# Four gate tiles of a delta-net mixer moved behind the scan, the scan's output kept in SBUF

## The chip, the cores and the metric

One core of one Trainium2 chip runs the whole program. The metric is the device time of one execution in microseconds (us); three runs of the kernel before gave 3149.6 us as median (3138.0 to 3154.76). TensorE (PE) multiplies, VectorE (DVE), ScalarE (ACT) and GpSimd (POOL) do the rest, SyncE (SP) issues most of the DMAs and POOL some.

## The reference

Two transformer blocks run one after the other on a sequence of 512 tokens, 1024 wide, in fp32. The first block has two layers, and each has a mixer and a feed-forward part. The change touches the mixer alone, so it is carried out twice. Cut to what matters:

```
h = rmsnorm(x, norm_mix_g[l]);  proj = h @ w_in[l]
(qa, ka, va, qd, kd, vd, beta_logit, decay_logit, z, gate_logit) = split(proj)
y_attn = grid_attention(qa, ka, va) @ w_o_attn[l]      # softmax attention, 8 heads, 2 kv heads

# gated delta rule, forward and backward in time, chunks of 64 tokens
t_inv = triangular_solve(eye + a_kk, eye)              # one 64x64 inverse per chunk and head
u, w, qk, q_dec, k_dec, g_tot = ...                    # from t_inv and the decays
def step(state, ...):                                  # 8 chunks, one after the other
    v_new = u - w @ state
    o     = q_dec @ state + qk @ v_new
    state = state * g_tot + k_dec.T @ v_new
o = rmsnorm(o_fwd + o_bwd, dn_out_norm_g[l]) * silu(z)
y_dn = o @ w_o_dn[l]

gates = sigmoid(gate_logit)                            # [2, 1024] per token
x = x + (gates[0] * y_attn + gates[1] * y_dn) @ w_out[l]
```

## The kernel before, in words

Activations lie feature-major: a tile `[128, 512]` holds 128 features of all 512 tokens. A product in fp32 is made of three passes over fp32r halves (hi x hi, hi x lo, lo x hi). A tile of 128 output columns from 1024 inputs is therefore 24 products of 128x512 on PE (`pg<-xh,wh`, `pg<-xh,wl`, `pg<-xl,wh`), and one from 512 inputs is 12. Weights come by DMA into `st`; ACT copies them to the high half `wh` and DVE or POOL subtracts to get the low half `wl`.

A gate tile (`g_tanh`) is such a tile of `gate_logit`: 24 products, a DVE step `tha<-pg,R`, a tanh on ACT into `thz` and a store to the DRAM tensor `thd` (L1261). A mixer has 16 of them, eight for attention's branch (pushed as "ga") and eight for the delta net's (pushed as "gd"). `push` puts generators into a background queue; `pull` takes work from it beside a foreground stream in a ratio (the list `R1`); `need(name)` runs all that is left under a name. So the gate tiles fill PE while the delta net's solve, a chain of small steps over ACT, DVE and PE, goes on.

Then the scan (`g_dn_scan`, over chunks, two groups of heads, both directions) and attention (`g_grid_attention`) run woven together. Attention's k, v and q come back from DRAM by POOL's queue (L823 to L829). At the end of attention stands its output product with `w_o_attn`, eight tiles of 12 products into the PSUM tiles `as` and `at` in turn. Each is multiplied by its gate (`gate`: load of `thz` from `thd`, L1338, and one DVE step into `s` or `sq`) and stored to the DRAM tensor `um` by SP (L853).

The scan adds its output into a tile `o`, stores it to the DRAM tensor `od` (L1213), and the output norm (`g_dn_out`) loads it again (L1218). The norm squares `o` on ACT, sums per head and token on PE (`pt<-c_ident,sq`), takes the inverse root on DVE (`oms`, `nw`, `nwb`, ending in `orr`), transposes it on PE (`pt<-c_ident,orr`), splits it into halves in `rr` (a zeroed tile, L1236), spreads it over the partitions on PE (`pt<-rr,selp`), multiplies by the gain and by `z`, and splits the result into `oh` and `ol`. The product with `w_o_dn` follows (`pg<-oh,wh`), eight tiles of 12, each gated, added to `u` (loaded from `um`, L1353) and split for `w_out`.

Within each engine instructions run in the order in which a scheduler has put them; the scheduler lays this order out from its own model of durations, so small edits in the code move instructions some way. A tile's buffers come from pools: a tag with two buffers lets two tiles of that tag live at once, and pools opened later may take the SBUF space of pools closed before.

Of the kernel before, what the change touches and what calls it, by code (L numbers as in the profile page):

```python
# [7 lines left out]
F32 = mybir.dt.float32  # L8
# [11 lines left out]
T = 512  # L20
# [86 lines left out]
class Net:  # L107
# [583 lines left out]
    def g_attn(self, pool, qk, v, hd, nkeys, mult, po, first=True, last=True, causal=False, extra=None):  # L691
# [4 lines left out]
        for t in range(NT):  # L696
# [21 lines left out]
            if m is not None:  # L718
                r2 = self.small(1, "ar2")
                self.tt(r2, ri, m, ALU.mult)  # L720
                ri = r2
            if t % SCALE_DVE[0] == SCALE_DVE[1]:
                self.V.tensor_scalar(p[:, 0:n], p[:, 0:n], ri, None, ALU.mult)
# [92 lines left out]
    def g_grid_attention(self, l, pool, qd, kd, vd, ad, gate, ud):  # L816


        for h in range(8):
            g, hs = h // 4, slice(64 * (h % 2), 64 * (h % 2) + 64)  # L820
            if h % 4 == 0:
                k = self.t(pool, [128, 2, T], "k", F32R, bufs=1)
                self.nc.gpsimd.dma_start(k, kd[:, g])  # L823
                vt = self.t(pool, [128, NT, 2, 64], "v", F32R, bufs=1)
                self.nc.gpsimd.dma_start(vt, vd[:, g])
                v = [(vt[:, t].rearrange("p u d -> p (u d)"),) for t in range(NT)]
            if h % 2 == 0:
                q = self.t(pool, [128, 2, T], "q", F32R)
                self.nc.gpsimd.dma_start(q, qd[:, h // 2])  # L829
                a = self.t(self.xp, [128, T], "sq")  # L830
            po = self.t(self.po, [128, T], "po")
            yield from self.g_attn(
                pool, self.pairs(q[:, h % 2], k[:, 0], k[:, 1]), v, 64, T, None, po
            )
            self.act(a[hs], po[64:128])
            self.tt(a[hs], a[hs], po[0:64], ALU.add)
            if h % 2 == 1 and h < 7:
                self.nc.sync.dma_start(ad[:, h // 2, :], a)
        o = []
        for n in ("ph", "pl"):  # L840
            x = [self.t(pool, [128, 2, T], n, F32R) for _ in range(2)]
            o.append([x[f // 2][:, f % 2] for f in range(4)])
        self.split(o[0][3], o[1][3], a)
        for f in range(3):
            a = self.t(pool, [128, T], "p", bufs=3)
            self.nc.sync.dma_start(a, ad[:, f, :])
            self.split(o[0][f], o[1][f], a)
        self.need("ga")

        def evac(f, ps):  # L850
            u = self.t(self.xp, [128, T], ("s1", "sq")[f % 2])
            gate(f, ps, u)
            self.nc.sync.dma_start(ud[:, f, :], u)  # L853

        yield from self.g_fm(
            self.I["w_o_attn"][l], 512, 0, D, *o, evac, 128,
            lambda f: self.t(self.ps[f % 2][0], [128, T], self.ps[f % 2][1]),
        )
# [249 lines left out]
    def g_dn_scan(self, l, pool, g, x, G, tt_, qk, od):  # L1108
# [1 line left out]

        beta3, fac, kds3, eg3, gt = G
        V = self.V
        o = self.t(pool, [128, 2, T], f"o{g}", bufs=1)
        half = [slice(0, 64), slice(64, 128)]
        S = None
        for i in range(NT):
# [32 lines left out]
            for n in (2 * i, 2 * i + 1):  # L1149
# [4 lines left out]
                for h in range(4):  # L1154
                    for d in range(2):
                        a = cs[d] % 2
# [5 lines left out]
                if n > 0:  # L1162
                    for par in range(2):
                        for hh in range(2):
                            for d in range(2):
                                a = cs[d] % 2
# [5 lines left out]
                if n < 7:  # L1172
                    for d in range(2):
                        a = cs[d] % 2
# [12 lines left out]
                if n > 0:  # L1187
                    for par in range(2):
                        for d in range(2):
                            a = cs[d] % 2  # L1190
# [4 lines left out]
                for d in range(2):  # L1195
                    a, t = cs[d] % 2, toks[d]
# [3 lines left out]
                for d in range(2):  # L1200
                    a = cs[d] % 2
                    dst = o[:, :, 64 * cs[d] : 64 * cs[d] + 64]
# [4 lines left out]
                    if n > 0:  # L1207
                        for par in range(2):
                            dp = dst[half[par]]
                            self.tt(dp, dp, X[par][half[par], 2 * d : 2 * d + 2], ALU.add)  # L1210
                if n < 7:
                    S = Sn
        self.nc.sync.dma_start(od[:, 2 * g : 2 * g + 2, :], o)  # L1213

    def g_dn_out(self, l, pool, g, zd, od, out):

        o = self.t(pool, [128, 2, T], "o")
        self.nc.sync.dma_start(o, od[:, 2 * g : 2 * g + 2, :])  # L1218
        ms = self.small(16, "oms", 2)
        m3 = ms.rearrange("p (t h) -> p t h", t=NT)  # L1220
        for hh in range(2):
            sq = self.t(pool, [128, T], "sq")
            self.act(sq, o[:, hh], AF.Square)
            ps = self.t(self.pt, [128, T], "pt")
            for t in range(NT):
                self.mm(ps[:, 2 * t : 2 * t + 2], sq[:, 128 * t : 128 * t + 128], self.blk2)
            self.V.tensor_copy(m3[:, :, 2 * hh : 2 * hh + 2], ps[:, 0:8].rearrange("p (t h) -> p t h", t=NT))
            yield 2.0
        self.V.tensor_scalar(ms, ms, 1.0 / 64, EPS, ALU.mult, ALU.add)
        r = self.small(16, "orr", 2)  # L1230
        self.rsqrt(r, ms)
        ps = self.t(self.pt, [128, T], "pt")
        for t in range(NT):
            self.tr(ps[0:4, 128 * t : 128 * t + 128], r[:, 4 * t : 4 * t + 4])
        rr = self.t(pool, [128, T], "rr", F32R)
        self.V.memset(rr.bitcast(F32), 0.0)  # L1236
        self.act(rr[0:4], ps[0:4])
        self.tt(rr[32:36], ps[0:4], rr[0:4].bitcast(F32), ALU.subtract)
        yield 3.0
        gcol = self.cols[:, 184 + l : 185 + l]  # L1240
        for hh in range(2):
            ps = self.t(self.pt, [128, T], "pt")
            self.mm(ps, self.selp[:, hh], rr)
            self.stt(o[:, hh], o[:, hh], gcol, ps, ALU.mult, ALU.mult)
            z = self.t(pool, [128, T], "z")
            self.nc.sync.dma_start(z, zd[:, 2 * g + hh, :])
            self.tt(o[:, hh], o[:, hh], z, ALU.mult)
            self.split(out[0][2 * g + hh], out[1][2 * g + hh], o[:, hh])
            yield 3.0
# [69 lines left out]
    def mixer(self, l):  # L1319
        self.last = deque(self.last, maxlen=LAG[0])  # L1320
        I = self.I
        w = I["w_in"][l]
        thd = self.t(self.dr, [128, 16, T], f"thd{l}")
        zd = self.zd
        od = self.t(self.dr, [128, 4, T], f"od{l}")
        ad = self.t(self.dr, [128, 4, T], f"ad{l}")
        ud = self.t(self.dr, [128, NK, T], f"um{l}")
        qd = self.t(self.dr, [128, 4, 2, T], f"qd{l}")
        kd = self.t(self.dr, [128, 2, 2, T], f"kd{l}")
        vd = self.t(self.dr, [128, 2, NT, 2, 64], f"vd{l}")  # L1330
        gp, gcm = self.pool(f"mix{l}", bufs=2)
        self.gp = gp
        self.follow()
        self.push("ga", *self.tanh_tiles(w, 2848, 8, lambda f: thd[:, f, :]))
        self.push("gd", *self.tanh_tiles(w, 2848 + 1024, 8, lambda f: thd[:, 8 + f, :]))
        def gate(f, ps, dst):
            th = self.t(gp, [128, T], "thz")
            self.nc.sync.dma_start(th, thd[:, f, :])  # L1338
            self.stt(dst, th, 1.0, ps, ALU.add, ALU.mult)

        inputs = self.g_grid_inputs(l, qd, kd, vd)
        self.delta_net(l, od, inputs, lambda pool: self.g_grid_attention(l, pool, qd, kd, vd, ad, gate, ud))
        self.need("z")
        pool, cm = self.pool(f"mo{l}", bufs=2)
        mx = self.f32r_tiles(pool, NK, "m")
        dp, dcm = self.pool(f"md{l}", bufs=2)
        self.selp = self.t(dp, [128, 2, 128], "selp", F32R, bufs=1)
        self.V.tensor_copy(self.selp.rearrange("p a b -> p (a b)"), self.const(dp, "selp", 128, 256, "z"))
        o = self.f32r_tiles(dp, 4, "o")

        def evac_d(f, ps):
            u = self.t(dp, [128, T], "u", bufs=4)
            self.nc.sync.dma_start(u, ud[:, f, :])  # L1353
            a = self.t(dp, [128, T], "sq")
            gate(8 + f, ps, a)
            self.tt(a, a, u, ALU.add)
            self.split(mx[0][f], mx[1][f], a)

        self.run(self.g_dn_out(l, dp, 0, zd, od, o), R1[5], (self.g_dn_out(l, dp, 1, zd, od, o), 1.0))
        self.need("gd")  # L1360
        self.gemm_fm(I["w_o_dn"][l], 512, 0, D, *o, evac_d)
        dcm.__exit__(None, None, None)
        self.residual(pool, I["w_out"][l], D, *mx, 0.5, self.col(1, l), lambda: self.begin_ffn(l))
        for c in (cm, gcm):
            c.__exit__(None, None, None)
# [503 lines left out]


SCALE_DVE = (2, 1)

R1 = [2.071, 0.633, 0.45, 3.49, 0.059, 9.505, 0.491, 4.55, 0.469, 0.387, 0.519, 0.788]
RATIO = [0.357, 0.101, 0.485, 1.137, 0.284, 0.392, 0.568]
# [53 lines left out]
```

## Time and profile before

| what | value |
|---|---|
| median of three runs | 3149.6 us |
| the profiled execution | 3150.24 us, of which its span 3148.4 us |
| PE busy | 3034.4 us, 96% of the span |
| DVE busy | 2224.4 us, 71% |
| ACT busy | 1502.1 us, 48% |
| POOL busy | 410.6 us, 13% |
| bytes moved by DMA | 371.35 MB, 118 GB/s on average |

The busy share is an average over very different stages, and matmuls overlap in it. The mixers take about 505 us (from 45 to 550) and 525 us (from 900 to 1425) of the span. The change acts at two places of each: in the first mixer from 268 to 310 us, where the solve ends and the scan begins, and from 424 to 478 us, where the scan ends and `w_o_attn`, the output norm and the first products of `w_o_dn` follow. In the second mixer the same places lie some 870 us later. Start times of PE's products of one shape show the clock: the same product starts at a shorter distance from the one before it when the clock is full. A row of a timeline gives the idle time ahead of an instruction in brackets, with what ended it.

### The profile page before, as it was taken

The page shows a single profiled execution, that of the slowest core. Times are in us where ns is not written, and L with a number is a line of the kernel's source. Part 1 is how long each engine was busy: PE and PEld are TensorE (multiplying, and loading weights), DVE is VectorE, ACT ScalarE, POOL GpSimd, SP SyncE. Part 2 cuts the span into 40 slices and gives each one's busy share as a digit, 9 for nine tenths or more (in the row PEclk, how much of TensorE's full clock was granted, in tenths as well). Part 3 has the DMA queues.
Part 4 walks back from the last instruction along what each step waited for, and adds up shares of the span by engine and source line. Part 5 has one row for each costly group of instructions (what it writes and reads, how often), then busy time and mean ns, then how long its engine had stood idle before and what let it go on. Part 6 is the DMA issues. An engine that isn't in the chain of part 4 may idle for free.

```text
span 3148.4 us, 54558 instructions
## 1 busy us (share of the span) xinstructions
PE 3034.4 (96%) x20156; PEld 2551.5 (81%) x20156; DVE 2224.4 (71%) x5004; ACT 1502.1 (48%) x3045; POOL 410.6 (13%) x548
## 2 busy tenths in 40 slices
PE   8989989999999999899999999999998999999998
PEld 6877778888888777788888898888986898888976
DVE  5987766777349887767773565788676566688674
ACT  4544644444235546444443443366464453376462
POOL 2433300000014333000000010200100010100200
PEclk9999999999999999999999999999999999999999
DMA  4435145333443351453333444422535444422525
GB/s 145 117 94 147 33 156 181 93 95 97 127 124 104 95 153 42 152 180 93 97 97 124 134 132 134 131 70 68 158 109 162 141 128 142 110 64 85 157 88 157
DMA packets 408877, 371.35 MB, mean 118 GB/s; under 512 B 33507, under 2 KB 351203, under 8 KB 408611
## 3 DMA queue, kind: packets, MB, share of 16 engines
q1 hardware_dynamic: 402467, 347.94, 37.9%
q0 software_dynamic: 6144, 19.93, 1.8%
q8 instruction: 159, 2.61, 0.4%
q14 instruction: 107, 0.88, 0.1%
HBM read 300.01 MB, written 67.76 MB: 117 GB/s over the span
## 4 chain that ended last, share of the span: by engine, by line
PE 81%; DVE 11%; DMA 4%; ACT 2%; issue 2%; POOL 0%; SPq 0%; DVEq 0%; ACTq 0%; POOLq 0%
PE pg L229 63%; PE pa L229 5%; PE po L229 4%; PE pt L240 3%; PE pt L229 3%; DVE e L243 2%; DVE cva L246 1%; PE as L229 1%; DVE wl L243 1%; PE at L240 1%; DVE pl L243 1%; DMA thz<-thd 1%; DMA thz<-th 1%; DVE anb L711 1%; DVE tha L246 0%
## 5 line engine op out<-in xcount | busy, mean ns | idle before, releaser
L249 ACT ACTIVATE wh<-st 128x512 fp32r<-128x512 f32 x844 | 527.8, 629 | 792.3 <-PE pg L229 605.9
L243 DVE TENSOR_TENSOR wl<-st,wh 128x512 fp32r<-128x512 f32 x766 | 531.8, 696 | 412.8 <-ACT wh L249 407.5
L229 PE MATMUL pg<-xh,wh 128*128 128x512 f32 (+1 forms) x1824 | 732.3, 402 | 6.5 <-DVE pad L243 2.8
L229 PE MATMUL pg<-xh,wl 128*128 128x512 f32 (+1 forms) x1824 | 720.9, 396 | 7.4 <-POOL wl L243 5.4
L229 PE MATMUL pg<-xl,wh 128*128 128x512 f32 (+1 forms) x1824 | 713.2, 396 | 0.0
L229 PEld LDWEIGHTS pg<-xh,wh 128*128 128x128 f32 (+1 forms) x1824 | 345.6, 189 | 76.4 <-DVE pad L243 3.2
L229 PEld LDWEIGHTS pg<-xh,wl 128*128 128x128 f32 (+1 forms) x1824 | 345.2, 189 | 76.0 <-POOL wl L243 7.0
L229 PEld LDWEIGHTS pg<-xl,wh 128*128 128x128 f32 (+1 forms) x1824 | 344.6, 189 | 74.9 <-issue 0.4
L229 PE MATMUL pg<-wh,xh 128*128 128x256 f32 x928 | 263.2, 288 | 5.4 <-DVE nw L266 3.2
L229 PE MATMUL pg<-wl,xh 128*128 128x256 f32 x928 | 264.4, 286 | 0.0
L229 PE MATMUL pg<-wh,xl 128*128 128x256 f32 x928 | 261.4, 284 | 0.0
L229 PEld LDWEIGHTS pg<-wh,xh 128*128 128x128 f32 x928 | 175.8, 191 | 11.6 <-ACT v L249 4.0
L229 PEld LDWEIGHTS pg<-wl,xh 128*128 128x128 f32 x928 | 177.3, 191 | 3.0
L229 PEld LDWEIGHTS pg<-wh,xl 128*128 128x128 f32 x928 | 176.6, 191 | 1.0
L474 POOL DMA_DIRECT2D xd<-xn x40 | 21.8, 545 | 1128.6 <-DVE xn L246 800.3
L243 POOL TENSOR_TENSOR wl<-st,wh 128x512 fp32r<-128x512 f32 x78 | 123.3, 1587 | 243.0 <-ACT wh L249 198.7
L229 PE MATMUL pg<-hh,wl 128*128 128x512 f32 x352 | 136.9, 389 | 0.0
L229 PE MATMUL pg<-hh,wh 128*128 128x512 f32 x352 | 136.6, 389 | 0.0
L249 ACT ACTIVATE p<-pa,anb 128x128 f32<-128x128 f32 (+1 forms) x224 | 115.5, 516 | 44.2 <-DVE anb L711 38.8
L229 PE MATMUL pg<-hl,wh 128*128 128x512 f32 x352 | 135.6, 389 | 0.0
L249 ACT ACTIVATE ph<-pt 128x128 fp32r<-128x128 f32 (+1 forms) x224 | 94.1, 427 | 75.1 <-PE pt L240 74.0
L229 PE MATMUL po<-ph,v 128*128 128x256 f32 x480 | 123.9, 285 | 6.1 <-ACT ph L249 6.1
(508 smaller groups left out, 6301.0 us busy)
## 6 DMA issues: line engine op xcount, KB each, us to landing
st<-in_w_in_dram SPq DMA_DIRECT2D x400, 256.0 KB
st<-in_w_up_dram SPq DMA_DIRECT2D x176, 256.0 KB
st<-in_w_down_dram SPq DMA_DIRECT2D x88, 256.0 KB
st<-in_w_out_dram SPq DMA_DIRECT2D x64, 256.0 KB
xo<-xd SPq DMA_DIRECT2D x48, 256.0 KB
th<-thz SPq DMA_DIRECT2D x48, 256.0 KB
thz<-th SPq DMA_DIRECT2D x48, 256.0 KB
xd<-xn POOLq DMA_DIRECT2D x40, 256.0 KB, 4.0
```

Source lines behind the costliest of these rows:

```text
L229: return self.pe(self.PE.matmul(out, lhsT, rhs, start=start, stop=stop, **kw))
L240: return self.pe(self.PE.transpose(out, in_, self.ident[0:k, 0:k]))
L243: return (eng or self.V).tensor_tensor(out, a, b, op)
L246: return self.V.scalar_tensor_tensor(out, a, s, b, op0, op1)
L249: return self.S.activation(out, in_, f, **kw)
L474: self.nc.gpsimd.dma_start(self.xd[:, k, :], x)
L711: self.V.tensor_reduce(nb, ps[:, 0:n], AX.X, ALU.max, negate=True)
```

## The change

Four gate tiles of the delta net's branch (`LATE = 4`, the last four of eight, 96 products of 128x512 a mixer) are pushed only after the scan, and the generators of the output norm run beside them; the ratio `R1[5] = 9.505` is the old one. The scan's output tiles `o0` and `o1` live in the mixer's own pool and are read from there, without the DRAM tensor `od`. The `um` stores are issued by POOL instead of SP. The zeroing of `rr` goes from DVE to POOL. The gate of the delta net's branch has its own four buffers `th` instead of the two of `thz`.

```diff
@@ g_grid_attention
             gate(f, ps, u)
-            self.nc.sync.dma_start(ud[:, f, :], u)
+            self.nc.gpsimd.dma_start(ud[:, f, :], u)
@@ g_dn_scan
-        o = self.t(pool, [128, 2, T], f"o{g}", bufs=1)
+        o = od[g]
...
-        self.nc.sync.dma_start(od[:, 2 * g : 2 * g + 2, :], o)
@@ g_dn_out
-        o = self.t(pool, [128, 2, T], "o")
-        self.nc.sync.dma_start(o, od[:, 2 * g : 2 * g + 2, :])
+        o = od[g]
...
-        self.V.memset(rr.bitcast(F32), 0.0)
+        self.G.memset(rr.bitcast(F32), 0.0)
@@ mixer
-        od = self.t(self.dr, [128, 4, T], f"od{l}")
+        od = [self.t(gp, [128, 2, T], f"o{g}", bufs=1) for g in range(2)]
...
-        self.push("gd", *self.tanh_tiles(w, 2848 + 1024, 8, lambda f: thd[:, 8 + f, :]))
-        def gate(f, ps, dst):
-            th = self.t(gp, [128, T], "thz")
+        gd = self.tanh_tiles(w, 2848 + 1024, 8, lambda f: thd[:, 8 + f, :])
+        self.push("gd", *gd[:LATE])
+        def gate(f, ps, dst, pool=gp, tag="thz", bufs=None):
+            th = self.t(pool, [128, T], tag, bufs=bufs)
...
         self.need("z")
+        self.need("gd")
+        self.push("gd", *gd[LATE:])
...
-            gate(8 + f, ps, a)
+            gate(8 + f, ps, a, dp, "th", 4)
...
+LATE = 4
```

What this does to the order of instructions is seen at three places of the first mixer; the second reads alike. The first is PE's queue where the solve ends and attention and the scan begin (`T` is the solve's inverse, `kq` decayed keys, `as<-k,q` attention's scores). Before:

```order
L229 MATMUL pg_3365<-xl_39_171,wh_3367 128x512
L229 MATMUL pg_3365<-xh_32_164,wh_3467 128x512
L229 MATMUL pg_3365<-xh_32_164,wl_3468 128x512
L229 MATMUL pg_3365<-xl_40_172,wh_3467 128x512
L229 MATMUL as_3485<-k_3475,q_3479 128x512 x2
L229 MATMUL pg_3365<-xh_33_165,wh_3467 128x512
L229 MATMUL pg_3365<-xh_33_165,wl_3468 128x512
L229 MATMUL pt_3395<-T_2728,kq_599_3385 64x64 x4
L229 MATMUL pa_3442<-T_2758,kq_611_3432 64x64 x4
```

The same place on PE in the changed kernel, up to the scan's first product (`pt<-tmv,T`):

```order
L229 MATMUL pa_3299<-T_2759,kq_579_3289 64x64 x4
L229 MATMUL as_3330<-k_3320,q_3324 128x512 x2
L229 MATMUL pt_3260<-T_2729,kq_565_3241 64x64 x4
L229 MATMUL pt_3260<-T_2729,kq_568_3249 64x64 x4
L229 MATMUL pa_3300<-T_2759,kq_576_3281 64x64 x4
L229 MATMUL pa_3300<-T_2759,kq_579_3289 64x64 x4
L240 MATMUL pt_3240<-c_ident_81,kq_570_3253 128x128 x2
L229 MATMUL as_3348<-k_3320,q_3324 128x512 x2
L229 MATMUL pt_3420<-tmv_1101,T_2729 64x64 x4
```

No gate product (`pg`) stands there any more: 96 of them have left the queue between the solve's last pieces and the scan.

The second place is PE's queue behind `w_o_attn`, where the output norm ends and `w_o_dn` begins (`at` is the last tile of `w_o_attn`). Before:

```order
L229 MATMUL at_5088<-ph_4861,wl_5091 128x512
L229 MATMUL at_5088<-pl_4863,wh_5090 128x512
L240 MATMUL pt_5721<-c_ident_81,orr_5707 4x128 x4
L229 MATMUL pt_5730<-rr_5702,selp_5632 128x512
L229 MATMUL pt_5738<-rr_5726,selp_5632 128x512
L229 MATMUL pt_5746<-rr_5702,selp_5632 128x512
L229 MATMUL pg_5762<-oh_1092_5636,wh_5765 128x512
```

After, from the last products of the last late gate tile (`pg_5608`) on:

```order
L229 MATMUL pg_5608<-xh_35_167,wl_5629 128x512
L229 MATMUL pg_5608<-xl_43_175,wh_5628 128x512
L229 MATMUL pt_5661<-c_ident_81,sq_5659 128x2 x4
L229 MATMUL pt_5669<-c_ident_81,sq_5667 128x2 x4
L240 MATMUL pt_5690<-c_ident_81,orr_5676 4x128 x4
L240 MATMUL pt_5714<-c_ident_81,orr_5700 4x128 x4
L229 MATMUL pt_5723<-rr_5695,selp_5461 128x512
L229 MATMUL pt_5731<-rr_5719,selp_5461 128x512
L229 MATMUL pt_5739<-rr_5695,selp_5461 128x512
L229 MATMUL pt_5747<-rr_5719,selp_5461 128x512
L229 MATMUL pg_5755<-oh_1055_5465,wh_5758 128x512
```

Before, the four norm groups stand between the tiles of `w_o_attn`. After, all 96 late gate products stand between `w_o_attn` and `w_o_dn`, with one norm group ahead of them, one before their last six, and the other two groups, both `orr` transposes and `rr` behind them.

The third place is SP's queue during `w_o_attn`. Before:

```order
L853 DMA um_93_382<-sq_4921 128x512
L1338 DMA thz_4970<-thd_90_379 128x512
L391 DMA st_5764<-in_w_o_dn_dram 128x2x256
L1353 DMA u_5800<-um_93_382 128x512
L1353 DMA u_5809<-um_93_382 128x512
L853 DMA um_93_382<-s_978_4945 128x512
L1338 DMA thz_5020<-thd_90_379 128x512
```

After:

```order
L1338 DMA thz_4777<-thd_90_379 128x512
L391 DMA st_4920<-in_w_o_attn_dram 128x4x128
L1338 DMA thz_4801<-thd_90_379 128x512
L391 DMA st_5483<-in_w_in_dram 128x4x128
L1338 DMA thz_4851<-thd_90_379 128x512
L391 DMA st_5501<-in_w_in_dram 128x4x128
```

The `um` stores have gone to POOL's queue, the `u` loads behind the last `thz` load, and weights of the late gate tiles (`in_w_in`) come between the `thz` loads.

## Rows read from the trace of the kernel before

**Rows 1.** The page, part 4, shares of the chain by engine.

```profile
PE 81%; DVE 11%; DMA 4%; ACT 2%; issue 2%; POOL 0%; SPq 0%; DVEq 0%; ACTq 0%; POOLq 0%
```

**Rows 2.** Stretches: length, busy by engine (instructions), granted clock, DMA share, GB/s.

```profile
268.00:290.00 22.00, 18.47 (x433) 13.95 (x432) 14.38 (x24) 17.27 (x29) 5.08 (x4) 0.84 0.39 103
290.00:310.00 20.00, 20.00 (x250) 15.73 (x248) 11.34 (x23) 8.67 (x16) 2.19 (x4) 1.00 0.76 232
...
424.00:444.00 20.00, 16.00 (x108) 13.10 (x105) 11.73 (x29) 6.94 (x12) 0.00 (x0) 0.83 0.72 243
444.00:466.00 22.00, 18.00 (x88) 14.17 (x87) 13.65 (x44) 5.00 (x9) 0.00 (x0) 0.96 0.79 265
466.00:478.00 12.00, 11.51 (x40) 8.62 (x40) 8.23 (x13) 3.52 (x6) 0.00 (x0) 0.79 0.30 87
478.00:546.00 68.00, 68.00 (x303) 56.34 (x302) 46.33 (x73) 30.13 (x50) 4.39 (x8) 1.00 0.63 198
...
1314.00:1336.00 22.00, 18.26 (x90) 14.66 (x89) 14.24 (x42) 4.85 (x8) 0.00 (x0) 0.97 0.88 283
```

**Rows 3.** Timeline of PE, front: start, length, line, operation, shape, [idle before].

```profile
281.55 0.63 PE L229 MATMUL pg<-xh,wl 128*128 128x512 f32 x1
281.98 0.63 PE L229 MATMUL pg<-xl,wh 128*128 128x512 f32 x1
...
293.86 0.39 PE L229 MATMUL pg<-xl,wh 128*128 128x512 f32 x1
294.09 0.40 PE L229 MATMUL pg<-xh,wh 128*128 128x512 f32 x1
...
311.78 0.56 PE L229 MATMUL pt<-tmv,T 64*64 64x64 f32 x6
```

**Rows 4.** Timeline of ACT, front.

```profile
281.38 2.53 ACT L249 ACTIVATE T<-fm 32x512 f32<-32x512 f32 x4
```

**Rows 5.** Timeline of DVE, front.

```profile
293.40 0.68 DVE L1102 COPY T<-pa 32x512 f32<-32x512 f32 x1 [0.50 <-PE pa L229]
```

**Rows 6.** Timeline of POOL, front.

```profile
293.90 0.58 POOL L823 DMA_DIRECT2D k<-kd  x1 [6.11 <-issue]
```

**Rows 7.** DMA issues from 290 to 300 us: KB each, us to landing.

```profile
q<-qd POOLq DMA_DIRECT2D x2, 512.0 KB, 6.5
...
k<-kd POOLq DMA_DIRECT2D x1, 512.0 KB, 4.2
```

**Rows 8.** Timeline of PE, tail: idle ends ahead of w_o_attn and w_o_dn.

```profile
431.23 0.80 PE L229 MATMUL as<-ph,wh 128*128 128x512 f32 x1 [4.00 <-ACT ph L249]
...
465.15 1.22 PE L229 MATMUL pt<-rr,selp 128*128 128x512 f32 x2 [3.18 <-DVE rr L243]
466.53 0.80 PE L229 MATMUL pg<-oh,wh 128*128 128x512 f32 x1 [0.16 <-ACT oh L249]
```

**Rows 9.** Timeline of PE, tail: one norm group inside w_o_attn.

```profile
446.80 0.95 PE L229 MATMUL pt<-c_ident,sq 128*128 128x2 f32 x8
447.61 0.49 PE L229 MATMUL as<-ph,wh 128*128 128x512 f32 x1
```

**Rows 10.** Chain of waits, tail: start, length, what.

```profile
444.58 5.93 DMA um<-s
...
451.37 4.09 DMA thz<-thd
...
456.75 5.56 DMA thz<-thd
```

**Rows 11.** Timeline of DVE, tail: steps of the norm.

```profile
448.46 0.17 DVE L1229 TENSOR_SCALAR oms<-oms 128x16 f32<-128x16 f32 x1
448.67 0.17 DVE L266 TENSOR_SCALAR nw<-oms 128x16 int32<-128x16 int32 x1
...
463.04 0.74 DVE L246 SCALAR_TENSOR_TENSOR o<-o,cols,pt 128x512 f32<-128x512 f32 x1
```

**Rows 12.** The page, part 6: a 256 KB store issued by POOL.

```profile
xd<-xn POOLq DMA_DIRECT2D x40, 256.0 KB, 4.0
```

## The prediction

> **What bounds the kernel now.** I read the page first: the chain that ended last is four fifths TensorE (PE), so a change pays only where PE stands idle, runs at its low clock or carries work that can go elsewhere [rows 1]. Then the table by stretch. In the first mixer PE is short of work in four of five stretches around the scan: 3.5 us idle and a granted clock of 0.84 in the 22 us ahead of it, none in the next 20 us, then 4.0, 4.0 and 0.5 us idle behind the scan, at granted clocks of 0.83, 0.96 and 0.79; the second mixer's tail is the same (18.26 of 22 us busy at 0.97) [rows 2]. The rest I took from the engines' timelines at the two places where the order changes: the front (the solve's end up to the scan's first product) and the tail (from the last product of scan and attention to the first product of w_o_dn).
>
> Two prices first. In the timeline of the front, products of 128x512 start 0.43 us apart where the clock is low and 0.23 us apart where it is full [rows 3]. Four gate tiles are 96 such products, 96 x 0.227 = 21.8 us per mixer at full clock. They are moved, not saved, so the sum is what their leaving gives at the front less what their arrival costs at the tail.
>
> **Front, removed.** Before, those 96 products fill PE between the solve's pieces; twelve of them stand in the low clock, which makes them 12 x 0.2 = 2.4 us dearer, so 24.2 us could go at most. But the scan also needs the solve, and that is a chain through ACT and DVE with little PE in it. ACT's last fm copies begin at 281.38 and take 2.53 us [rows 4], and what stands in front of them is nearly all the solve's own: a single wh cast goes. From there the chain goes on through short PE, ACT and DVE steps; in before they wait behind PE's backlog, so that the last T copy on DVE comes at 293.40, released by PE [rows 5]. By the durations alone, without the moved products, that copy comes near 288.0, 5.4 us sooner. The next thing needed is q and k for attention: POOL issues them at 293.90 and after [rows 6]; I put that at 288 to 289, and the transfers take 4.2 us (k) and 6.5 us (q, the median of two) [rows 7], so q lands near 295 and the first as product, which PE's order places ahead of most of the scan, waits for it. Behind it the scan's first product comes near 297.5 instead of 311.78 [rows 3]. Gain 14.3 us, an estimate from these rows. Bounds: 24.2 us if nothing but PE's backlog held the scan; 8 us if T copies and q come where they came, less only what stood after them. I take 14.3. What is late next is the q load. PE is then nearly empty for 10 us, so the scan starts at the low clock; the half-speed stretch of before lasted about 5 us for twelve products, 2.4 us lost [rows 3], and I charge 2.3 us. **Front: -12.0 us.**
>
> **Scan and attention.** Same work, a little reordered; both orders keep PE full there. Zero, with 3 us either way.
>
> **Tail, in before.** PE idles 4.00 us for the split of the last attention tile, starts w_o_attn at 431.23, so its work ended at 427.23, waits again 3.18 us for rr on DVE, and starts w_o_dn at 466.53 [rows 8]. That is 39.3 us. Inside w_o_attn stand four norm groups (`pt<-c_ident,sq`), each 0.81 us until the next product [rows 9].
>
> **Tail, after.** (1) The order now has attention's last `po` ahead of the scan's last products and four w_o_attn products between them, so the 4.00 us go and w_o_attn is 0.4 us in when the scan ends: -0.4. (2) w_o_attn is 96 products again, now without norm groups and at full clock: 21.9 us by the spacing. Each gate needs its thz load, issued when the gate two tiles back has released the buffer; in before such loads sat 4.09 and 5.56 us on the chain, and an um store 5.93 us, held there because u loads that wait for a store stand ahead of thz loads in SP's queue [rows 10]. After, um goes by POOL and no u load stands between them. A pair of tiles is 24 x 0.228 = 5.5 us of PE; a load of 4.1 to 5.6 us with 0.7 us of gate and 0.4 us of issue comes to 5.2 to 6.7 us. So the last gate, which holds the PSUM bank of the first late tile, ends at 22 to 26 us: I take 24. (3) The first Square waits for w_o_attn's last product, since its tile takes the attention's place in SBUF; Square and the first norm group are about a copy of that shape on ACT, a good half of a microsecond (four smaller copies take 2.53 us [rows 4]), 0.81 [rows 9] and hand-overs, 1.7 us, of which part hides behind that last gate; I keep all. (4) Ninety late gate products, the second group, six more: 21.8 us, their weights loaded during w_o_attn. (5) What is left of the norm comes after them and nothing fills PE: two groups 1.6, the copies and two interleaved rsqrt chains 2.5 (ten dependent steps 0.21 apart [rows 11]), the transposes and the ACT copy 1.4, two rr 1.4, then one selp product, stt 0.74 [rows 11], z multiply and oh cast (of the same 128x512 shape, a little shorter) with their hand-overs, together 2.6: 9.5 us. Sum: -0.4 + 24 + 1.7 + 21.8 + 9.5 = 56.6 us against 39.3. **Tail: +17.3 us**, 13 to 23.
>
> **The small edits.** o's round trip through DRAM goes (two stores, two loads of 512 KB a mixer); in before the Squares waited for it, but inside PE's work on w_o_attn, so alone it is worth 0 to 1 us. DMA moves 243 and 265 GB/s in the two tail stretches [rows 2], so w_o_attn's loads may land sooner; that stands in the bounds of (2). The rr memsets go to POOL, which is idle there (0.00 us busy from 424 to 466 [rows 2]): nothing; were it late, it would hold only rr. The gate's own four buffers let w_o_dn's th loads start early, where PE is full (68.00 of 68.00 us from 478 on [rows 2]): 0, at most 1 us.
>
> For the um stores the nearest row is POOL's store of the same 256 KB, 4.0 us from issue to landing [rows 12]. With 0.5 us of issue and 0.7 us of gate that is 5.2 us, just under the pair's 5.5 us, so the move costs nothing; at 6 us a landing it would hold w_o_attn by 5 us a mixer.
>
> The Trainium skill, "DMA: Bandwidth & Descriptors", section "Anatomy of one DMA", gives about 2.0 us plus the bytes over 436 GB/s for a DMA issued from GpSimd, 2.6 us for this size. The row of this kernel has 4.0, so the row decides. By the page the store's loop would be 3.8 us, never the pace, and I should give rival B below 0.18 rather than 0.24.
>
> **Sum.** -12.0 + 17.3 = +5.3 us a mixer, two mixers: +10.6 us on the profiled execution's 3150.24 us, 3160.8. The median of the runs shown, 3149.6, is 0.6 us under it, so on that scale 3160. About 0.5%, 15.7 us, is what a measurement of this kernel can tell from no change.
>
> **Rivals.**
> A, the front pays in full. For it: PE is full from 290 to 310 [rows 2], and the solve's late steps there are released by PE. Against it: q lands 4.2 to 6.5 us after its issue, whatever PE does. Then -24.2 + 2.3 at the front, and +12 at the tail if w_o_attn takes 21.9 and part of the norm hides: -10 a mixer, -20, 3130 us. It decides from a first scan product before 290.
>
> B, slower: w_o_attn is paced by its loads and stores. With six 256 KB transfers per pair of tiles (thz, um and late weights) in 5.5 us it asks for 286 GB/s, above what either tail stretch moved [rows 2]. If the pair takes 7.2 us, w_o_attn lasts 28.8, the norm 10.5 us, and the tail comes to 62.4, +23.1; with a front of only -9 + 2.3: +16.4 a mixer, +33, 3183 us. It decides from gates of one tile and the next but one standing over 6.8 us apart.
>
> C, the norm hides. The order holds its last groups behind the late gate products, but if their chain leaves only the 4 us of waiting that before shows, the tail is +12: 3150 us, no change. Against it: 9.5 us of dependent steps in that order.
>
> **Chances.** The sum as worked out 0.40 (its own range 3148 to 3172, of which 0.09 lies more than 15.7 us above before), A 0.24, B 0.24, C 0.12. Faster by over 0.5%: 0.24. Within 0.5%: 0.31 + 0.12 = 0.43. Slower: 0.24 + 0.09 = 0.33. The range reaches to A's 3130 and past B's time, with 3 us of the scan: 3128 to 3186.
>
> **What would show it.** Right: the scan's first product 12 to 17 us sooner after the solve's last fm copy, with PE idle before it and the q load as releaser; PE idle 8 to 11 us between the last late gate product and w_o_dn; 54 to 60 us from the scan's end to w_o_dn; no wait for thz over 2 us. Wrong: the scan starting 20 us sooner (A), gates over 6.8 us a pair (B), under 5 us idle ahead of w_o_dn (C), or a scan that itself changes by more than 3 us.

## The result, and the profile after

The changed kernel takes 3187.37 us (median of four runs, 3186.25 to 3192.15) against 3148.46 us before: ratio 1.013, 95% interval 1.0116 to 1.0144. It is 39 us slower. The forecast was 3160 us, inside the 15.7 us that the prediction counted as no change; its range ended at 3186. The profiled execution of after took 3186.29 us, its span 3184.2 us.

Where the 36 us between the two spans went is seen from five start times on PE in each mixer: the scan's first product (`pt<-tmv,T`), the last product of scan and attention, the first and the last of `w_o_attn`, the first of `w_o_dn`. Lengths below are differences of such starts, so they are a few tenths off those in the prediction, which began where the idle time began.

| us | before, 1st mixer | after | difference | before, 2nd mixer | after | difference |
|---|---|---|---|---|---|---|
| scan's first product | 311.78 | 301.90 | -9.9 | 1181.71 | 1193.67 | (below) |
| scan, first to last product | 115.2 | 124.1 | +9.0 | 115.7 | 120.7 | +5.0 |
| from there to `w_o_dn` | 39.6 | 56.5 | +16.9 | 39.4 | 63.8 | +24.4 |
| `w_o_dn`'s last product | 491.15 | 507.21 | +16.1 | 1361.48 | 1401.81 | +40.3 |

From `w_o_dn`'s last product in the first mixer to the scan's first in the second it is 690.6 us before and 686.5 after: -4.1 for the second front. Behind the second mixer's `w_o_dn` 4.5 us come back; that stretch, in which hardly anything was edited, takes between 1777.7 and 1786.9 us in the profiled executions of all the kernels below; why it varies was not traced.

The stretches of after at the front, in the scan, and behind it (length, busy by engine, granted clock, DMA share, GB/s) answer to [rows 2]:

```profile
268.00:290.00 22.00, 9.81 (x522) 8.09 (x520) 15.28 (x26) 16.16 (x27) 0.00 (x0) 0.61 0.37 114
290.00:302.00 12.00, 8.08 (x75) 5.66 (x76) 5.95 (x16) 4.44 (x10) 4.02 (x7) 0.50 0.56 171
302.00:307.00 5.00, 5.00 (x41) 3.78 (x44) 2.63 (x5) 2.89 (x7) 0.61 (x1) 0.50 0.00 0
307.00:426.00 119.00, 112.73 (x1678) 89.25 (x1675) 86.55 (x238) 77.29 (x181) 30.37 (x60) 1.00 0.10 31
```

PE was 18.47 of 22 us busy in the first of these before and is 9.81 now, but ACT is busy 16.16 us against 17.27: nearly all of ACT's work for the solve is still there, and PE waits for it at the low clock. The scan itself begins at the low clock (0.50 until 307).

The same chain in the timelines of after, one row each of ACT, DVE and POOL, against [rows 4 to 6]:

```profile
280.77 2.53 ACT L249 ACTIVATE T<-fm 32x512 f32<-32x512 f32 x4
```

```profile
289.60 0.68 DVE L1102 COPY T<-pa 32x512 f32<-32x512 f32 x1 [1.60 <-PE pa L229]
```

```profile
290.10 0.58 POOL L823 DMA_DIRECT2D k<-kd  x1 [23.00 <-PE pa L229]
```

ACT's step is 0.6 us sooner, DVE's 3.8, POOL's issue 3.8; and then, on PE:

```profile
297.40 1.19 PE L229 MATMUL as<-k,q 128*128 128x512 f32 x2 [1.66 <-DMA q<-qd]
...
300.76 1.20 PE L229 MATMUL as<-k,q 128*128 128x512 f32 x2
301.90 0.90 PE L229 MATMUL pt<-tmv,T 64*64 64x64 f32 x6
```

PE waits for the q load, as forecast, and needs 4.5 us from there to the scan's first product, at half clock (0.50 from 290 to 302).

In the second mixer less is gained. Counted from the start of ACT's last `fm` copies, the last T copy on ACT came 15.1 us later in before and comes 15.6 us later now (16.1 and 12.9 us in the first mixer). On the way to it PE stands still twice, 2.24 and 1.80 us, released by nothing that the profile shows ("issue"); in the first mixer there is one such pause, 1.63 us:

```profile
1177.28 0.48 PE L229 MATMUL pt<-fm,e 32*32 32x32 f32 x19 [2.24 <-issue]
```

The tail in PE's timeline of after, against [rows 8, 9]:

```profile
448.33 1.05 PE L229 MATMUL pt<-c_ident,sq 128*128 128x2 f32 x8 [0.77 <-ACT sq L249]
449.25 0.48 PE L229 MATMUL pg<-xh,wh 128*128 128x512 f32 x1
...
472.07 1.84 PE L229 MATMUL pt<-c_ident,sq 128*128 128x2 f32 x16
476.44 1.86 PE L240 MATMUL pt<-c_ident,orr 128*4 128x128 f32 x8 [2.53 <-DVE nw L246]
478.90 2.43 PE L229 MATMUL pt<-rr,selp 128*128 128x512 f32 x3 [0.60 <-DVE rr L243]
481.91 0.80 PE L229 MATMUL pt<-rr,selp 128*128 128x512 f32 x1 [0.59 <-DVE o L246]
482.50 0.63 PE L229 MATMUL pg<-oh,wh 128*128 128x512 f32 x1
```

Late gate products fill PE from 449.25 to 472.07; the norm's end then takes 10.4 us in the open, of which PE is idle 3.8 us and busy 6.66 us at a low clock:

```profile
472.07:482.50 10.43, 6.66 (x29) 3.99 (x28) 8.36 (x35) 3.06 (x5) 0.00 (x0) 0.61 0.16 58
```

In the second mixer the wait ahead of `w_o_attn` has stayed:

```profile
1318.65 0.80 PE L229 MATMUL as<-ph,wh 128*128 128x512 f32 x1 [4.01 <-ACT ph L249]
```

Loads and stores do not pace `w_o_attn`. On DVE of after, the gates of tiles 2 to 4 stand 2.6 and 2.5 us apart, with short waits (against [rows 10]), and POOL's um stores land about as its store in [rows 12] did (us to landing, from the DMA view of 424 to 452 us):

```profile
434.29 0.69 DVE L246 SCALAR_TENSOR_TENSOR s<-thz,as 128x512 f32<-128x512 f32 x1 [1.65 <-DMA um<-s]
...
436.91 0.69 DVE L246 SCALAR_TENSOR_TENSOR sq<-thz,at 128x512 f32<-128x512 f32 x1 [1.33 <-DMA thz<-thd]
...
439.44 0.69 DVE L246 SCALAR_TENSOR_TENSOR s<-thz,as 128x512 f32<-128x512 f32 x1 [1.24 <-PE as L229]
```

```profile
um<-s POOLq DMA_DIRECT2D x4, 256.0 KB, 3.6
um<-sq POOLq DMA_DIRECT2D x4, 256.0 KB, 4.3
```

### The profile page after: what moved, and what is told of

It is laid out like the page before. It is cut to its first block, busy times and chain, and to the rows that moved or that the text cites. A ratio compares the mean times of both kernels' runs of the same rounds, so it can differ in the third digit from the quotient of the medians.

```text
span 3184.2 us, 54578 instructions
## 1 busy us (share of the span) xinstructions
PE 3039.5 (95%) x20156; PEld 2553.8 (80%) x20156; DVE 2222.7 (70%) x5008; ACT 1506.6 (47%) x3045; POOL 408.7 (13%) x560
## 4 chain that ended last, share of the span: by engine, by line
PE 79%; DVE 12%; ACT 3%; DMA 3%; issue 2%; POOL 1%; SPq 0%; ACTq 0%; DVEq 0%; POOLq 0%
PE pg L229 61%; PE pa L229 5%; PE po L229 4%; PE pt L240 3%; PE pt L229 3%; DVE e L243 2%; PE as L229 2%; DVE cva L246 2%; DVE wl L243 1%; DVE anb L711 1%; ACT p L249 1%; DVE pl L243 1%; PE at L240 1%; PE at L229 1%; DMA thz<-th 1%
## 5 line engine op out<-in xcount | busy, mean ns | idle before, releaser
L243 POOL TENSOR_TENSOR wl<-st,wh 128x512 fp32r<-128x512 f32 x70 | 114.3, 1637 | 218.8 <-ACT wh L249 179.9
L249 ACT ACTIVATE p<-pa,anb 128x128 f32<-128x128 f32 (+1 forms) x224 | 115.6, 517 | 42.4 <-DVE anb L711 37.4
```

The costliest lines, as they stand in the source:

```text
L243: return (eng or self.V).tensor_tensor(out, a, b, op)
L249: return self.S.activation(out, in_, f, **kw)
```

## The experiments

Each was timed beside the kernel before on the same chip; the stages are read from one profiled execution of each. "Scan begins" is the start of the scan's first product in the first mixer; "scan" and "tail" are the second and third row of the table above, first and second mixer.

| kernel | median us | ratio to before (95%) | scan begins | scan | tail |
|---|---|---|---|---|---|
| before | 3144.5 to 3148.5 | 1 | 311.8 | 115.2, 115.7 | 39.6, 39.4 |
| after | 3187.4 | 1.0130 (1.0116 to 1.0144) | 301.9 | 124.1, 120.7 | 56.5, 63.8 |
| e1 own buffers alone | 3167.7 | 1.0068 (1.0052 to 1.0083) | 311.2 | 115.1, 115.9 | 48.2, 50.8 |
| e2 late tiles alone | 3179.8 | 1.0110 (1.0092 to 1.0128) | 302.7 | 124.2, 121.6 | 52.1, 56.3 |
| e3 after, shared buffers | 3172.9 | 1.0081 (1.0057 to 1.0105) | 302.6 | 128.4, 121.1 | 48.9, 57.8 |
| e4 after, none late | 3150.9 | 1.0015 (1.0003 to 1.0026) | 313.3 | 115.1, 115.4 | 43.6, 42.4 |
| e5 late tiles left out | 3142.6 | 0.9992 (0.9982 to 1.0002) | 302.5 | 126.6, 118.0 | 36.1, 43.2 |
| e6 front filled, late too | 3199.9 | 1.0176 (1.0161 to 1.0191) | 312.4 | 115.9, 115.6 | 64.0, 62.8 |
| e7 o in SBUF | 3133.4 | 0.9965 (0.9950 to 0.9979) | 313.3 | 115.2, 115.6 | 35.0, 35.1 |
| e8 the same, um on SP | 3138.3 | 0.9977 (0.9965 to 0.9988) | 311.5 | 115.3, 115.2 | 36.0, 35.5 |
| e9 PE filler in front | 3148.7 | 1.0011 (1.0002 to 1.0020) | 310.8 | 114.5, 115.0 | 41.8, 41.4 |
| e10 one own buffer | 3155.7 | 1.0033 (1.0020 to 1.0046) | 312.4 | 115.2, 115.5 | 38.9, 38.4 |
| e11 e7, one late | 3144.7 | 1.0002 (0.9990 to 1.0015) | 307.5 | 118.0, 123.5 | 43.1, 43.5 |
| e12 e7, two late | 3168.9 | 1.0073 (1.0058 to 1.0087) | 307.6 | 127.9, 122.1 | 44.8, 49.3 |

Two theories stood after the first comparison. One: the loss has two sources, an empty front that makes the scan slower, and own buffers that move the norm out of `w_o_attn`. The rival: all of it comes from the late tiles behind the scan.

**e1, own buffers alone**, in the kernel before:

```diff
-            gate(8 + f, ps, a)
+            gate(8 + f, ps, a, dp, "th", 4)
```

> The kernel before with one edit of the change alone: the delta net's gate in its own four buffers th. In the order this puts all four norm groups and both orr transposes behind the 96 products of w_o_attn, since the norm's tiles now take SBUF space that attention still holds. Theory (the buffers expose the norm): w_o_attn to w_o_dn goes from 35.3 us to 22.8 + 1.7 + about 13, so +2 to +6 us a mixer, 3152 to 3160 us. Rival (the loss is all in the moved gate tiles and the scan behind them): 3149, no change, within 5 us.

3167.7 us: more than the theory asked for, and far from the rival. The tail is 8.7 and 11.5 us longer. The four buffers take 8 KB a partition of the pool; behind them, as the order shows, the norm's tiles fall on space that attention holds. In e1 the load of `o` is issued only at 454.16, behind the last product of `w_o_attn` (453.36), and the Squares wait for the load; that `o` lies on attention's space too is read from this order:

```profile
459.45 0.63 ACT L249 ACTIVATE sq<-o 128x512 f32<-128x512 f32 x1 [5.04 <-DMA o<-od]
```

```profile
454.16 0.47 SPq L1218 DMA_DIRECT2D o<-od  x1
```

In before the first Square stands at 437.82, inside `w_o_attn`.

**e2, late tiles alone** (`LATE = 4` in the kernel before, nothing else of the change).

> The kernel before with LATE = 4 alone: o through DRAM, um stores on SP, the thz buffers as before. In the order three of the four norm parts stand inside w_o_attn again and only two selp products behind the late gate tiles. Theory: PE is full from the scan's end to w_o_dn, so the tail is 22.8 + 3.9 + 21.8 + 2 to 4 = 51 to 53 us against 55.9 in the changed kernel and 63.8 in its second mixer; with the front's and the scan's times of the changed kernel (about -1 and 0 us against before) 3149 + 2 x 12 = 3173, within 8. Rival (the norm's place does not matter, the moved tiles lose by the scan alone): 3187, as the changed kernel.

3179.8 us, within the theory's 8, but 7 us from the theory's 3173 and 7 from the rival's 3187: the sum does not decide between them. The tails are as forecast or longer (52.1, 56.3), and 4.4 and 7.5 us shorter than in after, so the norm's place matters; the scan is 9.0 and 5.9 us longer than in before, with no other edit in the kernel.

**e3, shared gate buffers**, the reverse of e1 in the changed kernel.

> The changed kernel with the gate of the delta net's branch back in the thz buffers; all other edits kept. Theory (the own buffers expose the norm): the norm's steps go inside w_o_attn, the late tiles cover its end, 8 to 14 us a mixer come back, 3160 to 3172 us. Rival: 3187, as the changed kernel.

3172.9 us, 14.5 us back, just above the range expected. The norm goes into `w_o_attn` again and the tail is 7.6 and 6.0 us shorter; the scan stays slow (128.4, 121.1).

**e4, none late** (`LATE = 8` in the changed kernel).

> The changed kernel with LATE = 8: no gate tile is moved, all other edits kept. The norm stands behind w_o_attn all the same. Theory: the front and the scan are those of before, and the exposed norm costs 2 to 6 us a mixer, 3152 to 3160. Rival (o in SBUF or the um stores on POOL slow the scan or w_o_attn): over 3165.

3150.9 us, just under the range given. Without late tiles the scan is that of before to 0.3 us, and the tail 3 to 4 us longer. Against e1 it is 17 us faster. `o` needs no load there, which is the likely reason; the um stores and the zeroing of `rr` differ too and were not separated.

**e5, late tiles left out** in both places, and **e6, front filled**: all eight early and the last four once more behind the scan.

```diff
# e5
-            self.nc.sync.dma_start(th, thd[:, f, :])
+            self.nc.sync.dma_start(th, thd[:, f - LATE if f >= 8 + LATE else f, :])
...
-        self.need("gd")
-        self.push("gd", *gd[LATE:])
# e6
-        self.push("gd", *gd[:LATE])
+        self.push("gd", *gd)
...
-        self.push("gd", *gd[LATE:])
+        td = self.t(self.dr, [128, 4, T], f"td{l}")
+        self.push("gd", *self.tanh_tiles(w, 2848 + 1024 + 128 * LATE, 8 - LATE, lambda f: td[:, f, :]))
```

> The changed kernel without the four late gate tiles at all: neither ahead of the scan nor behind it (the delta net's gates 4 to 7 read the tiles of gates 0 to 3 instead). Theory (an empty front makes the scan slower, whatever stands behind it): the scan's first product to its last keeps 120 to 125 us (before 115.2 and 115.7), the tail is that of the kernel with none late, 42 to 44 us, sum 3148 to 3158. Rival (the scan is slower because of the work queued behind it): 115.5 us for the scan and 3130 to 3138.

> The changed kernel with all eight gate tiles ahead of the scan, as before, and the last four computed a second time behind it into a scratch tensor nobody reads. Theory: the scan takes 115 to 116 us again, the tail 56 to 64 us as in the changed kernel; with the kernel that has none late at 3151 that is 3151 + 2 x 22 = 3195, 3190 to 3200. Rival (late work slows the scan): scan 120 to 125 us and over 3204.

This pair decides. In e5 nothing stands behind the scan, and the scan is still slow: 126.6 and 118.0 us. In e6 late work of the same size stands there, and the scan is 115.9 and 115.6. So it is the emptied front, with the clock and the order that come with it, and not the work behind. e5's scans missed the 120 to 125 us given on both sides; its sum, 3142.6, is below the 3148 expected, since its first tail is only 36.1 (the wait ahead of `w_o_attn` is gone there, as in after) and its second scan only 118.0. Taken together: 96 products a mixer left out altogether, with their weights and copies, are worth 8 us in the whole kernel (e4 against e5; 7 by the ratios) and not the 2 x 21.8 us of their PE time; the same 96 added behind the scan cost 49 us (e6 against e4).

**e7, o in SBUF** is the changed kernel with `LATE = 8` and the gate back in `thz`; **e8** has the um stores on SP besides.

> The changed kernel with LATE = 8 and the gate in the shared thz buffers: what stays of the change is o in SBUF, um stores on POOL and the rr zeroing on POOL. In the order the four norm groups, both orr transposes and all selp products stand inside w_o_attn. Theory (o in SBUF is worth what the round trip and the exposed norm cost): scan 115.5 us, the tail goes from 39.5 to 28 to 33 us, 3128 to 3138. Rival (the norm was hidden in w_o_attn in before already): 3142 to 3148.

> As e7_o_in_sbuf, but with the um stores on SP as before. Theory (the queue of the um stores costs nothing while PE is full): within 4 us of e7_o_in_sbuf. Rival (SP's u loads hold the thz loads, 5.9 us on the chain of before): 6 to 12 us slower than e7_o_in_sbuf.

e7 is faster than both kernels: 0.9965 of before, 12 us, at the upper end of its interval 0.9979 still clear of it, though less than the 0.5% that the prediction took as the least to be told. The norm now begins before `w_o_attn` (429.84, while PE waits for attention's last split) and its end is hidden:

```profile
429.84 1.05 PE L229 MATMUL pt<-c_ident,sq 128*128 128x2 f32 x8 [1.14 <-ACT sq L249]
431.21 2.82 PE L229 MATMUL pt<-c_ident,sq 128*128 128x2 f32 x16 [0.31 <-ACT sq L249]
...
463.39 0.47 PE L229 MATMUL pg<-oh,wh 128*128 128x512 f32 x1 [2.40 <-DVE sq L246]
```

The tail is 35 us, not the 28 to 33 expected; `w_o_attn` takes 26.5 us with the rest of the norm's products inside, and 2.4 us of waiting for the last gate remain. Beside the tail, `w_o_dn` itself is shorter, 22.2 us from first to last product against 24.6. e8's intervals overlap e7's; between 0 and 5 us for the um queue stays unclear.

**e9, PE filler**: e5 with 96 products on resident tiles in place of the gate tiles ahead of the scan, and one DVE copy of 8 columns for every 24 of them.

```diff
+    def g_fill(self):
+        ps = self.t(self.pg, [128, T], "pg")
...
+                self.mm(ps, self.xh[k][:, 0:128], x[k], start=(k + j == 0), stop=(k == nk - 1 and j == 2))
...
-        self.push("gd", *gd[:LATE])
+        self.push("gd", *gd[:LATE], *[self.g_fill() for _ in range(8 - LATE)])
```

> As e5_late_left_out (the four late tiles in neither place), but with 96 products of the same shape on resident tiles put in their place ahead of the scan: work for PE alone, without weights, casts or stores. Theory (what the scan misses is PE work in the front, which keeps the clock up and sets the order that the scheduler gives the scan): scan 115 to 117 us in both mixers, its start 7 to 11 us later than in e5_late_left_out, the sum within 6 us of it, 3137 to 3149. Rival (the casts or loads of the gate tiles matter): scan 118 to 126 us and 3150 or more.

The scan takes 114.5 and 115.0 us and begins 8.3 us later than in e5. Work that is nearly all PE's brings the scan back; casts and loads are not needed for it. The sum is 6.1 us above e5, at the edge of the 6 expected, though the filler is 2 x 21.8 us of PE time. Its front in the stretch view, at the full clock where e5 and after have 0.50:

```profile
268.00:290.00 22.00, 18.14 (x440) 14.63 (x439) 16.39 (x27) 15.85 (x27) 0.35 (x1) 0.92 0.35 111
290.00:310.00 20.00, 20.00 (x263) 15.84 (x262) 7.28 (x19) 4.42 (x10) 2.98 (x6) 1.00 0.36 106
310.00:315.00 5.00, 5.00 (x75) 3.85 (x75) 3.03 (x7) 3.95 (x12) 2.20 (x4) 1.00 0.01 3
```

**e10, one own buffer** (`dp, "th", 1` in e1).

> As e1_own_buffers, but with one own buffer instead of four. In the order the norm stands inside w_o_attn as before, since with one buffer the norm's tiles miss the space that attention holds. Theory (the price of the own buffers is where they push the norm's tiles): 3142 to 3150, as before. Rival (the gate in its own pool is slower in itself): 3160 to 3170, as e1_own_buffers.

3155.7 us, between the two. The norm stands inside `w_o_attn` and the tail is 38.9 and 38.4 us, which fits the space as the cause in e1. What I had missed is that a single buffer holds `w_o_dn`: from first to last product it takes 28.6 and 28.1 us, in before 24.6 in both mixers.

**e11 and e12**, one and two late tiles in e7 (`LATE = 7`, `LATE = 6`).

> As e7_o_in_sbuf with one gate tile late (LATE = 7). Theory (a late tile is paid in full behind the scan, and its place in the front gives back little): tail 35 + 5.5 = 40 us, front and scan together 0 to 4 us sooner, so +1 to +5 us a mixer, 3135 to 3144. Rival (one tile fits the 3 us that PE waits ahead of w_o_dn and the 4 to 5 us ahead of w_o_attn): 3125 to 3131.

> As e7_o_in_sbuf with two gate tiles late (LATE = 6). Theory: tail 35 + 10.9 = 46 us, front and scan together 0 to 6 us sooner, +5 to +11 us a mixer, 3143 to 3155. Rival (the dose does not count, only the exposed norm did): 3130 to 3137, as e7_o_in_sbuf.

3144.7 and 3168.9 us: e11 at the edge of its range, e12 far above. By the medians one tile costs 11 us over e7, two 36, four 40 (e3); by the ratios 12, 34 and about 36, so that two and four cannot be told apart. The two profiled executions lie only 13.4 us apart, since e11's took 3152.95 us, 8 above its median; between them the scans are 8.5 us longer and the tails 7.5. The longest scan is that of e12's first mixer, 127.9 us, and there the stretch view shows why:

```profile
297.00:307.00 10.00, 5.25 (x63) 3.83 (x62) 4.30 (x10) 3.97 (x10) 1.33 (x3) 0.70 0.77 249
307.00:312.00 5.00, 5.00 (x34) 3.56 (x32) 2.41 (x4) 3.28 (x8) 1.11 (x2) 0.50 0.05 19
312.00:317.00 5.00, 5.00 (x48) 3.52 (x46) 2.17 (x6) 2.79 (x7) 1.20 (x3) 0.50 0.01 3
317.00:337.00 20.00, 20.00 (x195) 15.87 (x194) 9.14 (x22) 7.73 (x20) 2.88 (x6) 0.55 0.00 1
337.00:377.00 40.00, 37.30 (x553) 29.62 (x551) 29.92 (x79) 26.76 (x68) 14.15 (x28) 1.00 0.16 48
```

PE idles half of the ten microseconds before the scan, the clock falls, and the scan's first 28 us run at about half of it although PE is busy all the time.

## Why the prediction was wrong

Front and scan together were to give back 12.0 us a mixer; they gave back 0.9 in the first and lost 0.9 in the second. That is 24 of the 25 us by which the spans' 36 us exceed the forecast 10.6; the second tail adds 7 more, and 5.5 come back in and behind the second `w_o_dn`.

**The step that failed** is the one on scan and attention: "Same work, a little reordered; both orders keep PE full there. Zero, with 3 us either way." It measured +9.0 and +5.0 us; the prediction had named such a change among its signs of being wrong. The other part is the size of the front, below. e2 and e5 show the slower scan with nothing else of the change and with no late work at all, e6 and e9 show it gone as soon as PE has work ahead of it. Of the 9.0 us in the first mixer, the rows account for 7.5. The clock: 5 us at 0.50 instead of 1.00, about 2.5 us; I had charged that to the front (2.3 us), so that part was only booked elsewhere. Four products of `w_o_attn` inside the scan: 0.9. Waits of PE: before, in the scan's whole length, 2.2 us idle; after, 6.3 us, 4.1 more:

```profile
311.80:427.00 115.20, 112.99 (x1717) 91.23 (x1716) 88.47 (x242) 76.40 (x184) 32.31 (x63) 1.00 0.13 39
```

against 112.73 of 119.00 in after's row above. The longest lists of PE's waits in after's scan are in attention's steps (products, busy us, mean ns, idle us before them):

```profile
L229 PE MATMUL as<-k,q 128*128 128x512 f32 x61 | 22.9, 456 | 1.4 <-ACT p L249 0.9 <-DMA k<-kd 0.3
L240 PE MATMUL at<-c_ident,p 128*128 128x128 f32 x128 | 20.4, 283 | 1.0 <-DVE pl L243 0.9
L229 PE MATMUL po<-ph,v 128*128 128x256 f32 x64 | 18.1, 305 | 1.1 <-ACT ph L249 1.0
```

The same three in before:

```profile
L229 PE MATMUL as<-k,q 128*128 128x512 f32 x60 | 21.9, 445 | 0.3 <-ACT p L249 0.3
L240 PE MATMUL at<-c_ident,p 128*128 128x128 f32 x125 | 19.7, 279 | 0.7 <-DVE pl L243 0.5 <-PE pt L229 0.2
L229 PE MATMUL po<-ph,v 128*128 128x256 f32 x64 | 17.5, 298 | 0.0
```

That is 3.5 us against 1.0, and most of it waits for the softmax's steps on ACT and DVE (`p`, `ph`, `pl`). The scheduler has interleaved scan and attention in another order than before; that this order covers those steps less is read from the waits.

Clock and order can be told apart in two other traces. In e11's first mixer, with one late tile, PE is busy 11.75 of the 12 us ahead of the scan at the full clock, and the scan is still 2.8 us longer than in e7, with 6.2 us idle:

```profile
295.50:307.50 12.00, 11.75 (x107) 9.07 (x105) 9.38 (x21) 6.39 (x14) 3.37 (x6) 1.00 0.81 242
307.50:425.50 118.00, 111.76 (x1719) 90.09 (x1718) 87.43 (x240) 78.48 (x185) 32.51 (x65) 0.99 0.13 40
```

And e3's first scan has the same 6.3 us idle as after's but stays at 0.50 for 12 us instead of 5 (row in the last section), and is 4.3 us longer. So the other order is worth about 4 us of waits, with a full front too, and the low clock comes on top, up to half of the time that it lasts. What remains of the 9.0 us, 1.5, is open, and so is which part of the front's work decides the scheduler's order.

**Front**, -14.3 us before the clock's charge: -9.9 in the first mixer and -4.1 in the second. The mechanism was right (q's load released PE), the size was not. In the first mixer q came at 297.4 instead of 295, and the way from there to the scan took 4.5 us at half clock instead of 2.5. The second mixer was taken to be like the first, and there the term is 10 us off: in before the scan began 27.8 us after the last `fm` copies had started, not 30.4, and after the change q released PE 19.0 us after them, against 16.6 in the first mixer and 13.6 in the forecast, since the T copies came no sooner. Why PE pauses there (the "issue" row above) stays open. Rival A, the front pays in full, is out.

**Tail**, +17.3: +16.9 in the first mixer, by nearly the parts given, whose errors cancel: late tiles 449.25 to 472.07, 22.8 us with one norm group, against 21.8; the open end of the norm 10.4 against 9.5; but from the scan's last product to that of `w_o_attn` only 21.1 against 23.6. In the second it is +24.4: step (1), that attention's last `po` comes ahead of the scan's end, holds in the first mixer's order only (there four products of `w_o_attn` stand inside the scan), and the statement ahead of the prediction that the second reads alike is wrong there. The 4.0 us of waiting stayed.

**The small edits** were mis-sized, and hidden inside the tail. "The gate's own four buffers ... 0, at most 1 us" a mixer: over both mixers they cost 21 to 23 us in e1 (by the ratio and by the medians), 14.5 in after (e3) and 17 between e4 and e7. "o's round trip ... 0 to 1 us" a mixer: in e7 and e8 its removal, together with the zeroing of `rr` on POOL, is worth 7 to 12 us over both; the rows show the norm beginning while PE still waits for attention, and the share of `rr` was not separated. I had read from the order that the norm stood behind the late tiles and priced it, but took it for a consequence of the moved tiles; it comes from the buffers (e1, e3).

**Rival B**, `w_o_attn` paced by its loads, did not happen, though its time (3183) came closest: the gates of one tile and the next but one stand 4.6 to 5.6 us apart, not 6.8. The um stores on POOL landed in 3.6 and 4.3 us, near the row of 4.0 that I had used and not the 2.6 that the Trainium skill's "DMA: Bandwidth & Descriptors", section "Anatomy of one DMA", makes of this size, an estimate from its figures. **Rival C** is out by its time, since 10.4 us stayed open and not 4. Its sign, under 5 us idle ahead of `w_o_dn`, was badly chosen: PE was idle only 3.8 of the 10.4 us, since its own steps of the norm, at a granted clock of 0.61, filled the rest. The 3 us of range given to the scan were a guess, from no row.

## What to carry to other kernels

Work that fills the slots of a latency-bound chain is nearly free where it stands: here 21.8 us of products a mixer gave back about 4 us where they left (e4 against e5) and cost about 25 where they went (e6 against e4). Look behind such a stage too: the next one can begin at a lower clock (after, e3, e12), and the scheduler can lay it out in another order (e11). Read both places where a change acts, not one: the second mixer's front gave 4 us where the first gave 10. And price a new buffer by what it pushes: ask which tiles move onto space that is still held, and who waits for them.

## What the runs showed of the hardware

PE busy in every slice does not bring the clock back at once: in e12 it stays at 0.50 to 0.55 for 28 us with PE 30.00 of 30 us busy, in after it returns within 5 us of the scan's start with the same busy share. In between lie e3, with 12 us, and e11's second mixer, with 16 us from the scan's start:

```profile
302.50:314.50 12.00, 12.00 (x103) 9.05 (x103) 6.15 (x14) 6.65 (x17) 2.21 (x5) 0.50 0.00 0
1179.40:1195.20 15.80, 15.80 (x150) 12.88 (x150) 5.92 (x15) 7.97 (x22) 2.12 (x5) 0.50 0.06 20
```

What decides how long it stays low, no run here shows. The distances between starts of one product confirm the clock of e12, 0.21 us for 128x256 at 320 and 0.12 us at 340:

```profile
319.98 0.41 PE L229 MATMUL po<-ph,v 128*128 128x256 f32 x1
320.19 0.41 PE L229 MATMUL po<-pl,v 128*64 128x256 f32 x1
...
339.67 0.28 PE L229 MATMUL po<-pl,v 128*64 128x256 f32 x1
339.79 0.28 PE L229 MATMUL po<-ph,v 128*128 128x256 f32 x1
```

The Trainium skill, "TensorE: Matmul & The Clock Gate", section "Seeing it yourself", warns that a trace's records of the clock gate can be unreliable on this chip and that the gate has been seen stuck low. These rows show half the clock, not the lower level that the page names, and here the matmuls' own spacing bears the record out.
